# A run-time branch of an expert stage, moved ahead of the last products of two expert pairs

## The chip, the core and the metric

The kernel runs on one core of a Trainium2 chip. Its time is the device time of one execution in microseconds (us); several executions are timed and their median is given. Engines are named as in the profile: PE multiplies matrices (PEld loads its stationary operand), DVE and ACT work on vectors, POOL is the fourth engine, and SP issues most of the loads. Each engine runs its own list of instructions in order; they meet through semaphores. All loads of weights go from HBM through 16 DMA engines.

## What is computed

The program computes two transformer blocks on 256 tokens of width 1024. The part that matters here is the last one, a mixture of experts: each token goes to 2 of 16 experts, and each expert has a hidden width of 512.

```python
def hier_moe(h, w_rg, b_rg, w_re, b_re, w1, w3, w2):
    ...
    def expert_step(acc, xs):
        w1e, w3e, w2e, ge = xs
        y = (jax.nn.silu(t @ w1e) * (t @ w3e)) @ w2e
        return acc + ge[:, None] * y, None

    acc, _ = lax.scan(expert_step, jnp.zeros_like(t), (w1, w3, w2, gates))
    return acc.reshape(b, n, d)
...
        x_lat = x_lat + g2 * hier_moe(h2_l, ...)
    return rmsnorm(x_lat, final_g)
```

## The kernel before

The kernel is one long program that a scheduler has put in order; the expert stage at its end is written in a fixed order (a manual schedule for PE; the others follow the order of the code). It takes the experts in 8 pairs; pair p is the experts 2p and 2p+1, each on 64 of PE's 128 columns. Every expert has 64 places for tokens. Tokens are gathered into these places by products with one-hot matrices (`gather`, for two pairs at a time) and brought back in the same way (`back` transposes the one-hot matrix, `scatter` and its `add` multiply with it and add to x).

For each pair the loop in `_body` (from `for p in range(8)`, L2051) issues on PE:

- `gate(p)`: the product with the pair's gate weights into `pg`; ACT makes `hp` of it (L1908, Silu).
- `down(p - 1)`: the product of the pair before with its down weights into two halves of `yacc`; `scatter(p - 1)` then has DVE multiply each half into `yf` (L1938), ACT round it to `yh` (L1939), and DVE keep the rest in `yl` (L1940).
- `up(p)`: the product with the up weights into `pu`; DVE multiplies it into `hp` (L1913).
- `back(p)`: two transposes (L1883), which DVE copies to `back` (L1884).
- `add()`: the products with `yh` and `yl` of the pair before (L1946, L1947), which DVE adds to x (L1948).
- `hidden_T`: four transposes of `hp` (L1920), which ACT copies to `hT` (L1921), the operand of `down(p)`.

The weights come as f32 in pieces of 1 MB, four for each product. `load_rows` (L250) issues them on SP into 14 buffers used in turn (`rawa`, `raw`, `rawb` and the tile `K01`, which the profile prints as K). A load waits until the products that read its buffer before are done, and until the load that used the same one of eight semaphores (DMAHW0 to DMAHW7, in turn) has landed. A product waits for the semaphore of each piece. In the text (7,0), (7,1) and (7,2) are the four loads of pair 7's gate, up and down weights; (6,2) are those of pair 6's down weights.

If an expert gets more than 64 tokens, a general path (`overflow`) computes the excess. Whether it is needed is known only at run time: the count `novi` is read into a register on every engine (L1960), and every engine branches on it (L1961). With the inputs used here the path is not taken. The path uses the tiles `yf`, `yh`, `hp`, `hT` and `few` of the pool that `scatter` uses too (four buffers of 128x1024 in turn), and ACT issues its loads into `few`. Where it is not taken, each engine adjusts its own semaphores as if it had been: it waits until its semaphore has reached the value that it has before the branch, and adds what the path would have added. SP does this for DMAHW0 to DMAHW7, one after the other.

In the kernel before, the branch stands in the last turn of the loop, behind `hidden_T` of pair 7 and ahead of `down(7)`. Just ahead of it the four loads of (7,2) are issued, so that they are in the queue when SP comes to the branch. After the loop follow `down(7)`, the scatter of pair 7, and the final normalisation (from L2076).

Of the kernel before, what the change touches and what calls it, by code (L numbers as in the profile page):

```python
# [117 lines left out]
def _body(tc, nc, es, I, out, dbg, stop, R):  # L118
# [28 lines left out]
    def alloc(kind, w, name, dt, tag=None):  # L147
        if kind == "2" and P.get("ffn2"):
            return a2(name, dt)
        t = (P["tag"].get(P["s"], P["s"]) if tag is None else tag) + kind  # L150
        if t not in P["b"]:
            t = kind
        return P["pool"].tile([128, w], dt, name=name, tag="k" + t, bufs=P["b"][t])

    def t4(name, dt=F32, tag=None):
        return alloc("4", 1024, name, dt, tag)
# [14 lines left out]
    def pa(name):  # L171
        t = pp.tile([128, 512], F32, name=name, tag="A", bufs=4)
        return t
# [11 lines left out]
    def pc2(name, t=None):  # L185

        if t is None:
            P["n2"] += 1
            t = "CD"[P["n2"] % 2]
        if P["pairs"]:  # L190
            t = pc(name, t)
            return [t[:, 0:512], t[:, 512:1024]]
        return [P["psum"].tile([128, 512], F32, name=name, tag=f"{t}{n}", bufs=1) for n in range(2)]
# [17 lines left out]
    def f32(ap):  # L211
        return ap.bitcast(F32)
# [25 lines left out]
    def load_rows(src, k):  # L238

        n, i = R["raws"], nraw[0] % sum(R["raws"])  # L240
        if i < n[0]:
            raw = P["raw1"].tile([128, 2048], F32, name="rawa", tag="rawa", bufs=n[0])
        elif i < n[0] + n[1]:
            raw = raw_tile()
        elif i == sum(n) - 1:
            raw = K01
        else:
            raw = P["raw2"].tile([128, 2048], F32, name="rawb", tag="rawb", bufs=n[2])
        nraw[0] += 1
        nc.sync.dma_start(raw, src.rearrange("(p k) n -> p (k n)", k=k))  # L250
        return raw
# [1446 lines left out]
    for i in range(4):  # L1698
# [5 lines left out]
        for f in range(2):  # L1704
            k, yf = 2 * i + f, ya[:, 256 * f:256 * f + 256]
# [172 lines left out]
    def back(p):  # L1878

        t = backs[p] = t1("back", F32R)  # L1880
        ps = pa("oht")
        for b in range(2):
            PE.transpose(ps[:, 128 * b:128 * b + 128], f32(oh[b][:, 128 * p:128 * p + 128]), ident)  # L1883
        DVE.tensor_copy(t, ps[:, 0:256])  # L1884
# [6 lines left out]
    ahead = {}  # L1891

    def fetch(p, i):
        n = 512 if i < 2 else 256
        return [[load_rows(experts[i][2 * p + u][n * h:n * h + n], n // 128) for u in range(2)] for h in range(2)]

    def product(p, i, ps):
        raws = ahead.pop((p, i), None) or fetch(p, i)
        for h, raw in enumerate(raws):
            for j in range(4):  # L1900
                k = 4 * h + j
                pair_mm(ps, xe[p](k), [r[:, 512 * j:512 * j + 512] for r in raw], k == 0, k == 7)

    def gate(p):
        ps = pa("pg")
        product(p, 0, ps)
        hps[p] = alloc("h", 512, "hp", F32, "")
        ACT.activation(hps[p], ps, AF.Silu)  # L1908

    def up(p):  # L1910
        ps = pa("pu")
        product(p, 1, ps)
        DVE.scalar_tensor_tensor(hps[p], ps, gsl[:, p:p + 1], hps[p], op0=OP.mult, op1=OP.mult)  # L1913

    def hidden_T(hp, t):

        ps = pa("eT")
        for f in range(4):
            o = 256 * (f // 2) + f % 2
            PE.transpose(ps[:, 128 * f:128 * f + 128], hp[:, o:256 * (f // 2) + 256:2], ident)  # L1920
        ACT.activation(t, ps, AF.Copy)  # L1921
        return t

    def down(p):
        yaccs[p] = pc2("yacc")
        raws = ahead.pop((p, 2), None) or fetch(p, 2)
        steps = [(f, n) for f in range(4) for n in range(2)]
        if p == 7:
            steps[4:] = [(2, 0), (3, 0), (2, 1), (3, 1)]
        for f, n in steps:  # L1930
            o = 1024 * (f % 2) + 512 * n
            pair_mm(yaccs[p][n], hTs[p][:, 128 * f:128 * f + 128], [r[:, o:o + 512] for r in raws[f // 2]], f == 0, f == 3)

    def scatter(p):

        yf, yh_, yl_ = t4("yf"), t4("yh", F32R), t4("yl", F32R)
        for n in range(2):
            tt(part(yf, n), yaccs[p][n], part(g2b, n), op=OP.mult)  # L1938
            ACT.activation(part(yh_, n), part(yf, n), AF.Copy)  # L1939
            tt(part(yl_, n), part(yf, n), f32(part(yh_, n)), op=OP.subtract)  # L1940

        def add():
            for n in range(2):
                for b in range(2):
                    r, ps = backs[p][:, 128 * b:128 * b + 128], pa("scat")
                    mm(ps, r, part(yh_, n), start=True, stop=False)  # L1946
                    mm(ps, r, part(yl_, n), start=False, stop=True)  # L1947
                    tt(part(x[b], n), part(x[b], n), ps, op=OP.add)  # L1948

        return add  # L1950

    def overflow():

        def some(w, k, i, n):

            t = t4("few")
            nc.scalar.dma_start(t.rearrange("p (k n) -> p k n", k=n), w.rearrange("(p k) n -> p k n", k=k)[:, i:i + n])
            return t

        nov = nc.values_load(novi, min_val=0, max_val=512)  # L1960
        with tc.If(nov > 0):  # L1961
            e_ = mybir.EngineType
            with tc.manual_schedule(engines={e_.PE, e_.DVE, e_.Activation, e_.Pool, e_.SP}):
                for b in range(2):
                    t, xT = t4("yf"), t4("yh")
                    tt(t, f32(xnh[b]), f32(xnl[b]), op=OP.add)
                    for k in range(8):
                        ps = pa("gat")
                        PE.transpose(ps[:, 0:128], t[:, 128 * k:128 * k + 128], ident)
                        DVE.tensor_scalar(xT[:, 128 * k:128 * k + 128], ps[:, 0:128], sc2p[:, k:k + 1], sh2p[:, k:k + 1],  # L1970
                                          op0=OP.mult, op1=OP.add)
                    acc = pc2("yacc")
                    for e in range(16):
                        hp = part(t4("hp"), 0)
                        for i in range(2):
                            ps = pa("pg")
                            for k in range(8):
                                if k % 2 == 0:
                                    raw = some(experts[i][e][512 * (k // 4):512 * (k // 4) + 512], 4, k % 4, 2)
                                mm(ps, xT[:, 128 * k:128 * k + 128], part(raw, k % 2), start=k == 0, stop=k == 7)  # L1980
                            if i:
                                DVE.scalar_tensor_tensor(hp, ps, gov[:, b, e:e + 1], hp, op0=OP.mult, op1=OP.mult)
                            else:
                                ACT.activation(hp, ps, AF.Silu)
                        hT = hidden_T(hp, part(t4("hT"), 0))
                        for f in range(4):
                            raw = some(experts[2][e][256 * (f // 2):256 * (f // 2) + 256], 2, f % 2, 1)
                            for n in range(2):
                                mm(acc[n], hT[:, 128 * f:128 * f + 128], part(raw, n), start=e + f == 0, stop=e == 15 and f == 3)
                    t = t4("yf")  # L1990
                    for n in range(2):
                        tt(part(t, n), acc[n], part(g2b, n), op=OP.mult)
                        tt(part(x[b], n), part(x[b], n), part(t, n), op=OP.add)
# [55 lines left out]
    with tc.manual_schedule(engines={mybir.EngineType.PE}):  # L2049
        add = None  # L2050
        for p in range(8):  # L2051
            gate(p)
            if p:
                down(p - 1)
                add = scatter(p - 1)
            else:
                places()
            up(p)
            if p % 2 and p < 7:
                gather(p + 1)  # L2060
            back(p)
            if add:
                add()
            hTs[p] = hidden_T(hps[p], alloc("h", 512, "hT", F32, ""))
            if p == 7:
                ahead[7, 2] = fetch(7, 2)
                overflow()
        down(7)
        scatter(7)()

# [66 lines left out]
```

## Time and profile before

| | us |
|---|---|
| median of 3 runs | 1166.79 |
| lowest and highest run | 1160.59, 1168.51 |
| the profiled execution | 1166.33 |
| its span, first to last instruction | 1164.6 |
| PE busy in the span | 1099.5 (94%) |
| DVE busy | 656.5 (56%) |
| ACT busy | 513.0 (44%) |
| POOL busy | 61.9 (5%) |
| mean granted clock of PE | 0.98 |

The times of the rows below are those of the profiled execution, in us from the start of its span. A row of a timeline has the start, the duration, the engine, the line, the operation, what it writes and reads, shapes, and the number of instructions merged in it; in brackets stands the idle time of the engine before it and what ended it. A "q" behind an engine's name is its sequencer, which waits, branches and issues.

### The profile page before, as it was taken

Reading aid. Unit: us, or ns where it says so; the run is one execution under the profiler, and the core shown is the slowest. Engines: PE = TensorE matmul, PEld = TensorE weight load, DVE = VectorE, ACT = ScalarE, POOL = GpSimd, SP = SyncE. Lnnn points to the kernel's source line nnn. Section 1 sums busy time; section 2 is a strip of 40 time slices with the busy share of each in tenths; the row PEclk is TensorE's granted clock in tenths of the full one; section 3 lists DMA queues with packets and bytes.
Section 4 is the critical chain, followed back from the end, with each engine's and each line's share of the span. In section 5 each row is a group of like instructions: output and inputs, shape, how many; then the busy total and the mean of one; then the engine's idle time right before and its main releaser. Section 6 shows DMA issues by size and latency. Waiting matters only on the chain. (4 is left out here: it accounts for less than half of the span.)

```text
span 1164.6 us, 16858 instructions
## 1 busy us (share of the span) xinstructions
PE 1099.5 (94%) x6823; PEld 834.5 (72%) x6823; DVE 656.5 (56%) x1050; ACT 513.0 (44%) x847; POOL 61.9 (5%) x106
## 2 busy tenths in 40 slices
PE   6999999998988999999999999999899899999994
PEld 5888887987765787888888688888799734343432
DVE  5656666555886566666566775656646603332323
ACT  5555554575563355555555444655544400100002
POOL 1000001000230011000000100000000300000000
PEclk9999999998999999999999999999999899999997
DMA  9855654553466737655565555313385699999992
GB/s 327 296 190 182 207 187 148 164 168 112 149 232 226 232 127 275 212 183 180 187 210 189 166 179 163 109 55 113 113 314 188 250 371 420 422 420 420 421 421 102
DMA packets 119534, 262.90 MB, mean 226 GB/s; under 512 B 6873, under 2 KB 83802, under 8 KB 105242
## 3 DMA queue, kind: packets, MB, share of 16 engines
q1 hardware_dynamic: 118506, 258.88, 61.8%
q0 software_dynamic: 656, 2.36, 0.5%
q8 instruction: 55, 0.90, 0.3%
q10 hardware_dynamic: 288, 0.52, 0.1%
q14 instruction: 29, 0.24, 0.1%
HBM read 260.70 MB, written 1.05 MB: 225 GB/s over the span
## 5 line engine op out<-in xcount | busy, mean ns | idle before, releaser
L268 DVE TENSOR_TENSOR lo<-raw,hi 128x1024 fp32r<-128x1024 f32 x243 | 297.2, 1224 | 213.7 <-ACT hi L267 213.4
L267 ACT ACTIVATE hi<-raw 128x1024 fp32r<-128x1024 f32 x246 | 260.2, 1058 | 213.5 <-PE pj L230 66.5
L308 PE MATMUL pj<-H,hi 128*128 128x512 f32 x352 | 122.1, 396 | 0.4 <-DVE H L599 0.4
L308 PE MATMUL pj<-hT,hi 128*128 128x512 f32 x352 | 122.0, 394 | 0.5 <-DVE hT L538 0.5
L229 PE MATMUL pj<-H,hi 128*128 128x256 f32 x400 | 117.6, 294 | 0.0
L231 PE MATMUL pj<-H,lo 128*128 128x256 f32 x400 | 113.6, 284 | 0.0
L230 PE MATMUL pj<-H,hi 128*128 128x256 f32 x400 | 113.6, 284 | 0.0
L311 PE MATMUL pj<-hT,lo 128*128 128x256 f32 x352 | 91.6, 281 | 0.0
L311 PE MATMUL pj<-H,lo 128*128 128x256 f32 x352 | 91.5, 281 | 0.0
L229 PEld LDWEIGHTS pj<-H,hi 128*128 128x128 f32 x400 | 76.9, 192 | 7.5 <-issue 4.4
L230 PEld LDWEIGHTS pj<-H,hi 128*128 128x128 f32 x400 | 76.9, 192 | 0.5 <-issue 0.5
L231 PEld LDWEIGHTS pj<-H,lo 128*128 128x128 f32 x400 | 76.8, 192 | 0.4 <-issue 0.3
L308 PEld LDWEIGHTS pj<-hT,hi 128*128 128x128 f32 x352 | 63.6, 188 | 13.3 <-DVE hT L538 1.5
L308 PEld LDWEIGHTS pj<-H,hi 128*128 128x128 f32 x352 | 64.1, 190 | 12.4 <-DVE H L599 0.8
L311 PEld LDWEIGHTS pj<-H,lo 128*128 128x128 f32 x352 | 66.8, 190 | 3.9
L311 PEld LDWEIGHTS pj<-hT,lo 128*128 128x128 f32 x352 | 66.2, 188 | 4.1
L1938 DVE TENSOR_TENSOR yf<-yacc,K 128x512 f32<-128x512 f32 x16 | 11.1, 691 | 100.0 <-PE yacc L1889 100.0
L423 PE MATMUL acc<-hi,hTh 128*128 128x512 f32 x160 | 62.7, 392 | 0.0
L424 PE MATMUL acc<-lo,hTh 128*128 128x512 f32 x160 | 62.7, 392 | 0.0
L427 PE MATMUL acc<-hi,hTl 128*128 128x512 f32 x160 | 49.8, 392 | 0.0
L1921 ACT ACTIVATE hT<-eT 128x512 f32<-128x512 f32 x8 | 4.8, 597 | 93.3 <-PE eT L1920 93.3
L647 ACT ACTIVATE gs<-pj 128x256 f32<-128x256 f32 x44 | 16.9, 384 | 44.3 <-PE pj L308 44.2
(518 smaller groups left out, 2113.2 us busy)
## 6 DMA issues: line engine op xcount, KB each, us to landing
raw<-in_w_in_dram SPq DMA_DIRECT2D x43, 1024.0 KB, 5.2
raw<-in_ffn_up_dram SPq DMA_DIRECT2D x22, 1024.0 KB, 5.5
raw<-in_ffn_down_dram SPq DMA_DIRECT2D x22, 1024.0 KB, 5.0
raw<-in_ffn_gate_dram SPq DMA_DIRECT2D x21, 1024.0 KB, 5.3
raw<-in_w_mod_dram SPq DMA_DIRECT2D x15, 1024.0 KB, 5.2
rawa<-in_w_exp_gate_dram SPq DMA_DIRECT2D x14, 1024.0 KB, 15.3
rawa<-in_w_exp_up_dram SPq DMA_DIRECT2D x11, 1024.0 KB, 13.2
raw<-in_w_exp_up_dram SPq DMA_DIRECT2D x11, 1024.0 KB, 19.8
```

Source lines behind the costliest of these rows:

```text
L229: mm(o, l[0], r[0], start=first, stop=False)
L230: mm(o, l[0], r[1], start=False, stop=False)
L231: mm(o, l[1], r[0], start=False, stop=last)
L267: ACT.activation(hi, r, AF.Copy)
L268: low = lambda: (sub or DVE).tensor_tensor(lo, r, f32(hi), op=OP.subtract)
L308: high = lambda: mm(ps, wh[:, s_], hl2(k), start=k == 0, stop=k == 7)
L311: mm(ps[:, 0:256], wl[:, s_], hl2.h(k), start=False, stop=False)
L423: mm(ps[b][n], hh, wh[:, s_], start=first and f == 0, stop=False)
L424: mm(ps[b][n], hh, wl[:, s_], start=False, stop=False)
L427: mm(ps[b][n], ll, wh[:, s_], start=False, stop=last and f == 1)
L647: ACT.activation(t, a, AF.Copy)
L1938: tt(part(yf, n), yaccs[p][n], part(g2b, n), op=OP.mult)
```

## The change

The branch and the loads move to an earlier place in the last turn of the loop: behind `gate(7)`, ahead of `down(6)` and `up(7)`. Since all loads issued later than the branch would come behind it in SP's list, the loads of (6,2) and (7,1) are issued ahead of it too, by a table that `down` and `product` read (`ahead`). Nothing else is changed.

```diff
         for p in range(8):
             gate(p)
+            if p == 7:
+
+                ahead.update({k: fetch(*k) for k in ((6, 2), (7, 1), (7, 2))})
+                overflow()
             if p:
                 down(p - 1)
                 add = scatter(p - 1)
...
             hTs[p] = hidden_T(hps[p], alloc("h", 512, "hT", F32, ""))
-            if p == 7:
-                ahead[7, 2] = fetch(7, 2)
-                overflow()
         down(7)
         scatter(7)()
```

On PE the branch stands, in the kernel before, behind the transposes `eT` of pair 7; L1969 is the general path's first instruction:

```order
L1946 MATMUL scat<-yh,back 128x512 [waits DVE_49]
L1947 MATMUL scat<-yl,back 128x512
L1920 MATMUL eT<-ident,hp 128x128 [waits DVE_49]
L1920 MATMUL eT<-ident,hp 128x128 x3
L1960 TENSOR_LOAD novi [waits DVE_49]
L1961 COMPARE_AND_BRANCH
L1969 MATMUL gat<-ident,yf 128x128 [waits DVE_49]
```

In the changed kernel it stands on PE behind the last products `pg` of pair 7's gate:

```order
L1889 MATMUL pg<-K_79,xe 64x512
L1889 MATMUL pg<-rawb,xe 64x512
L1889 MATMUL pg<-K_79,xe 64x512
L1960 TENSOR_LOAD novi [waits DVE_49]
L1961 COMPARE_AND_BRANCH
L1969 MATMUL gat<-ident,yf 128x128 [waits DVE_49,PE_49,Activation_49]
```

So the products of down(6) and up(7), the transposes of the one-hot matrix, the eight scatter products of pair 6 and the four transposes `eT` have moved from ahead of the branch to behind it.

On DVE, in the kernel before, the whole scatter of pair 6 stands ahead of the branch, and `yf` of that pair waits for PE alone:

```order
L1938 TENSOR_TENSOR yf<-yacc,K_81 128x512 [waits PE_49] x2
L1940 TENSOR_TENSOR yl<-yf,yh 128x512 [waits Activation_49] x2
L1913 SCALAR_TENSOR_TENSOR hp<-pu,gsl,hp 128x512 [waits PE_49]
L1884 CAST back<-oht 128x256 [waits PE_49]
L1948 TENSOR_TENSOR x_70<-x_70,scat 128x512 [waits PE_49]
L1948 TENSOR_TENSOR x_72<-x_72,scat 128x512 [waits PE_49]
L1948 TENSOR_TENSOR x_70<-x_70,scat 128x512 [waits PE_49]
L1948 TENSOR_TENSOR x_72<-x_72,scat 128x512 [waits PE_49]
L1960 TENSOR_LOAD novi [waits DVE_49]
L1961 COMPARE_AND_BRANCH
```

In the changed kernel the same rows of DVE stand behind the end of the general path (its two last branches are the first rows here):

```order
L1961 UNCONDITIONAL_BRANCH
L1961 UNCONDITIONAL_BRANCH [waits DVE_49]
L1938 TENSOR_TENSOR yf<-yacc,K_81 128x512 [waits DMAHW3_49,DMAHW4_49,DMAHW1_49,DMAHW5_49,DVE_49,DMAHW6_49,PE_49,Activation_49]
L1938 TENSOR_TENSOR yf<-yacc,K_81 128x512 [waits PE_49]
L1940 TENSOR_TENSOR yl<-yf,yh 128x512 [waits DMAHW6_49,DMAHW3_49,Activation_49]
L1940 TENSOR_TENSOR yl<-yf,yh 128x512 [waits Activation_49]
L1913 SCALAR_TENSOR_TENSOR hp<-pu,gsl,hp 128x512 [waits PE_49]
L1884 CAST back<-oht 128x256 [waits PE_49]
L1948 TENSOR_TENSOR x_70<-x_70,scat 128x512 [waits PE_49]
L1948 TENSOR_TENSOR x_72<-x_72,scat 128x512 [waits PE_49]
```

The first `yf` behind the branch takes on waits for five of the eight load semaphores; the first `yh` behind it, on ACT, waits for all eight. In the program built from the changed kernel the value that `yf` asks of DMAHW6 is 1264; each load adds 16, the 34 loads on that semaphore reach 544, and SP's adjustment at the branch adds 768. In the kernel before, the same waits stand at `yf` and `yh` of pair 7. On SP the rows are the same in both kernels.

## Rows read from the trace of the kernel before

**Rows 1.** The page, the span in 40 equal slices.

```profile
DMA  9855654553466737655565555313385699999992
GB/s 327 296 190 182 207 187 148 164 168 112 149 232 226 232 127 275 212 183 180 187 210 189 166 179 163 109 55 113 113 314 188 250 371 420 422 420 420 421 421 102
```

**Rows 2.** Stretches: length, busy us of PE, PEld, DVE, ACT, POOL; clock; DMA; GB/s.

```profile
1135.50:1138.30 2.80, 2.77 (x15) 2.23 (x14) 2.69 (x5) 0.00 (x0) 0.00 (x0) 1.00 1.01 418
1138.30:1142.50 4.20, 0.00 (x0) 0.00 (x0) 0.78 (x2) 0.60 (x1) 0.00 (x0) 0.99 0.43 174
1142.50:1146.00 3.50, 3.46 (x10) 1.22 (x12) 0.00 (x0) 0.00 (x0) 0.00 (x0) 0.53 0.03 7
```

**Rows 3.** Timeline of PE around the branch.

```profile
1137.64 0.63 PE L1920 MATMUL eT<-ident,hp 128*128 128x128 f32 x4
1142.55 1.08 PE L1889 MATMUL yacc<-raw,hT 128*64 128x512 f32 x1 [4.27 <-PEq L1961]
...
1143.42 1.06 PE L1889 MATMUL yacc<-raw,hT 128*64 128x512 f32 x1
...
1147.20 4.03 PE L1889 MATMUL yacc<-rawb,hT 128*64 128x512 f32 x17
```

**Rows 4.** The branch's lines, every engine: durations in ns min/median/max, first and last start.

```profile
L1961 SPq EVENT_SEMAPHORE  x8: 17/17/17, 1126.9 to 1141.9; - x8
...
L1961 SPq COMPARE_BRANCH  x1: 45/45/45, 1122.9 to 1122.9; - x1
L1961 PEldq COMPARE_BRANCH  x1: 4287/4287/4287, 1137.9 to 1137.9; - x1
...
L1961 ACTq COMPARE_BRANCH  x1: 50/50/50, 1138.8 to 1138.8; - x1
...
L1961 ACTq EVENT_SEMAPHORE  x1: 17/17/17, 1141.7 to 1141.7; - x1
...
L1960 PEldq TENSOR_LOAD <-novi x1: 488/488/488, 1137.3 to 1137.3; - x1
```

**Rows 5.** SP's last three loads: their issue; KB each, median us to landing.

```profile
1117.01 5.31 SPq L250 DMA_DIRECT2D rawb<-in_w_exp_down_dram  x3
...
rawb<-in_w_exp_down_dram SPq DMA_DIRECT2D x3, 1024.0 KB, 19.8
```

**Rows 6.** Timeline of PE: first and last row of gate(7), the end of up(7).

```profile
1110.62 4.08 PE L1889 MATMUL pg<-rawb,xe 128*64 128x512 f32 x17
...
1117.12 0.59 PE L1889 MATMUL pg<-K,xe 128*64 128x512 f32 x1
...
1131.93 3.65 PE L1889 MATMUL pu<-raw,xe 128*64 128x512 f32 x14 [1.33 <-SPq L1961]
```

**Rows 7.** Timeline of ACT: hT of pair 7.

```profile
1138.31 0.60 ACT L1921 ACTIVATE hT<-eT 128x512 f32<-128x512 f32 x1 [11.30 <-PE eT L1920]
```

**Rows 8.** Timelines of DVE, PE and ACT: from hp to hT of pair 6.

```profile
1108.07 0.75 DVE L1913 SCALAR_TENSOR_TENSOR hp<-pu,gsl,hp 128x512 f32<-128x512 f32 x1 [4.79 <-PE pu L1889]
...
1109.07 2.47 DVE L1948 TENSOR_TENSOR x<-x,scat 128x512 f32<-128x512 f32 x4
...
1110.06 0.63 PE L1920 MATMUL eT<-ident,hp 128*128 128x128 f32 x4
...
1110.73 0.60 ACT L1921 ACTIVATE hT<-eT 128x512 f32<-128x512 f32 x1 [8.17 <-PE eT L1920]
```

**Rows 9.** DVE and ACT, scatter of pair 6, then of pair 7; DVE's events at yf.

```profile
1124.79 0.69 DVE L1938 TENSOR_TENSOR yf<-yacc,K 128x512 f32<-128x512 f32 x1 [13.25 <-PE yacc L1889]
...
1149.61 0.69 DVE L1938 TENSOR_TENSOR yf<-yacc,K 128x512 f32<-128x512 f32 x1 [10.52 <-PE yacc L1889]
1150.99 0.69 DVE L1940 TENSOR_TENSOR yl<-yf,yh 128x512 fp32r<-128x512 f32 x1 [0.70 <-ACT yh L1939]
...
1150.33 0.63 ACT L1939 ACTIVATE yh<-yf 128x512 fp32r<-128x512 f32 x1 [11.43 <-DVE yf L1938]
...
L1938 DVEq EVENT_SEMAPHORE  x4: 21/50/7695, 1139.2 to 1141.9; - x4
```

## Prediction

> **What bounds the kernel now.** I read the page's slices first, then the end of the kernel in stretches, then the timelines of each engine around the branch, and last the rows of the branch line itself. A busy PE tells little here; the DMA row tells more: it stands at 9 tenths and about 420 GB/s from slice 33 to slice 39, and only the last slice falls to 102 GB/s [rows 1]. So the expert stage runs at the pace of its loads, and what can be won there is what stands after the last load. [...]
>
> The gap is the branch. PE's timeline has the last transposes of pair 7 at 1137.64 to 1138.27, then nothing until the first product of down(7) at 1142.55, an idle time of 4.27 us put down to PE's own sequencer at L1961; after it the first pair of matmuls takes 0.87 us (1142.55 to 1143.42), and down(7)'s last matmul ends at 1151.23, 13.4 us before the span's end [rows 3]. The branch line explains it: PE's compare-and-branch lasts 4.29 us. The same table has eight semaphore events on SP that run from 1126.9 to 1141.9 [rows 4]. They matter below.
>
> **What the change moves, part by part.**
>
> The loads. SP's list holds the same loads in the same order before and after: (7,0), (6,2), (7,1), (7,2), then the branch. The last three are issued from 1117.01 on and take 19.8 us to land; the third of them is issued at 1122.0 (the row's end, 1122.3, less one issue of 0.3), so it lands at 1141.8 [rows 5]. They wait for buffers that gate(7) and earlier products free, all ahead of either place of the branch. Nothing is gained or lost here: 0 us.
>
> The branch on PE. [...] Where it goes away it gives back the gap, up to the wait that is next: hT(7) on ACT would end at 1138.91 [rows 7], and down(7) could start at about 1139.0. Where it is added, behind it stand down(6), up(7), the back transposes, the scatter products of pair 6 and the transposes of pair 7. At most it costs 4.4 us of gap and the 1.6 us that down(7) pays now for the low clock (1142.55 to 1151.23 is 8.68 us, against 7.1): down(6) from 1122.1 to 1130.8, up(7) to 1137.9. At least it costs nothing, because the sequencer can run ahead of the array: in [rows 4] its load of the count starts at 1137.3, before the transposes that stand ahead of it have started at 1137.64. Both ends lie before 1144.6, where up(7)'s result is first wanted (next part), so I take 0 us in either case. The cover is that wait; without it the upper end would be 2.4 us, since up(7) now ends at 1135.6 [rows 6].
>
> The branch on ACT and DVE. ACT's takes 2.9 us (1138.8 to its event at 1141.7) [rows 4] and would come behind Silu(7), some 0.7 us after the end of gate(7) at 1117.71: done by about 1121.5, before anything needs ACT. DVE's comes behind the adds that end at 1111.54 [rows 8]; if it took ACT's 2.9 us, it would be past before gate(7) ends. 0 us for both.
>
> The correction of the semaphores. This is the part that decides. A branch that isn't taken must leave every semaphore where the taken one would leave it. SP does that for the eight load semaphores: it waits until each has counted all loads issued before the branch, in the order 0 to 7, and adds what the path not taken would have added. That is why its eight events end at 1141.9, with the last landing [rows 4]. Whatever comes behind the branch and reuses a buffer of the general path waits for the corrected values. The order shows which: yf on DVE waits for semaphores 3, 4, 1, 5 and 6, yh on ACT for all eight. In the kernel before, these were yf and yh of pair 7, which had to wait for down(7) anyway: DVE's four events at yf lie from 1139.2 to 1141.9 and the last one, 7.7 us long, then waits for PE [rows 9]. In the changed kernel the first to reuse such a buffer is yf of pair 6. It starts now at 1124.79 [rows 9]; semaphore 6 is corrected at 1141.8, so it will start at about 1141.95, some 17 us later.
>
> Behind yf on DVE are queued, strictly in turn, the second yf, two yl, the product hp(7) with the gate, the cast of back(7) and the four adds. PE's scatter products wait for yh and yl, its transposes of pair 7 for hp, ACT's hT for them, and down(7) for hT. The sum from 1141.95, each step by the rows of before:
> - yf to yh 0.72, yh to yl 0.66 (1149.61, 1150.33, 1150.99) [rows 9]; the second yf fills in, yh follows it, and the second yl starts at 1143.95; a DVE operation of this size starts 0.6 after the one before it (four adds in 2.47 us, [rows 8]), so hp starts at 1144.57.
> - [...] But PE will have idled from the end of up(7) to the first yh, some 6 to 8 us, longer than the 4.27 us after which it is granted 0.53 now. [...] I take the low clock here, because this is a longer idle time followed by thinner work than in [rows 2]: 1148.9.
> - down(7): 0.07 to its start, 7.1 at full clock, 8.68 with a whole low stretch like now. I take one slow pair, 7.5: the end at 1156.5. Bounds: 1155.0 (full clock throughout) and 1157.7 (the low stretch of now again).
> - The 13.4 us behind it are unchanged: the same rows in the same order, and pair 6's adds, done by about 1149, are out of the way.
>
> The end of down(7) moves from 1151.23 to 1156.5: **+5.3 us**, between +3.8 and +6.5. The profiled execution took 1166.33 us around a span of 1164.6, so 1171.6; the median of the three runs is 1166.79, 0.46 above it, which I don't add since the runs lie between 1160.59 and 1168.51. I forecast 1171.5 us.
>
> **The rivals.**
>
> *Faster: the corrected values don't hold the scatter.* If yf(6) runs when down(6) is done, as now, only the gap goes: down(7) starts at 1139.0, its second half needs the load of 1141.8 at about 1142.5, and it ends at 1146.1 instead of 1151.23: -5.1 us, 1161.2 us. For it speaks that SP passes its own compare already at 1122.9 [rows 4] and that the products themselves wait only for their own loads. Against it: the waits stand in the order, DVE's four events at yf are in the trace of before, and the value for semaphore 6 can't be reached by loads alone. It decides from the point where semaphore 6 is corrected before about 1124.8, which needs the last load 17 us earlier. [...]
>
> *Much slower: the branch in the middle of saturated loads.* At 1117 up to eight loads are queued, where at 1138 two were left. If the fetch at the branch's target had to wait behind all of them, it would return some 20 us later (the 19.8 us of [rows 5]), at about 1139.6; then down(6) 8.7, up(7) 7.1, 3.3 to hT and down(7) 7.1 follow: 1165.8, +14.6 us, 1180.9 us. For it: both share the DMA engines. Against it: PE's branch took 4.29 us although DMA still moved at 418 GB/s until 1138.3 and 174 GB/s on average after it [rows 2]. It decides from a fetch longer than about 11 us; shorter ones hide in the wait for yf(6). [...]
>
> **How the numbers follow.** The wait for the corrected semaphores is written in the program, and the rows give every step behind it: 0.86. The faster rival 0.08, the much slower one 0.06. About 1%, 11.7 us, is what a measurement of this kernel can tell from no change. The forecast with its +3.8 to +6.5 lies within it, as does the faster rival; the scatter of the runs (7.9 us from lowest to highest) puts a little of each over the edge. So faster by over 1% 0.02, within 1% 0.89, slower 0.09, most of that from the second rival. The range is 1171.5 with its bounds, 1170.1 to 1172.8, widened by the scatter of the runs on both sides: 1165.0 to 1177.0, which leaves out both rivals.
>
> **What would show it.** Right: in the changed kernel DVE's yf(6) starts within 0.3 us of the last of SP's eight events, near 1142; PE has no gap over 1 us between gate(7) and down(6) or one that ends before up(7) is wanted, but one of 5 to 8 us between the back transposes and the first scatter product, with the low clock behind it; down(7) starts near 1149 and the span ends near 1170. Wrong: yf(6) near 1125 and a span near 1159.5 (the first rival), or PE's compare-and-branch over 11 us (the second). If the gap behind the back transposes is there but down(7) starts before 1147, the step on the low clock was wrong.

## The result and the profile after

The changed kernel takes 1171.91 us (median of 15 runs, 1170.43 to 1177.03), the kernel before, run beside it, 1167.71 us (15 runs, 1160.24 to 1170.49). The ratio is 1.0057, with a 95% interval of 1.0040 to 1.0073: 6.7 us more (1167.7 times 0.0057), between 4.7 and 8.5. The ratio is an estimate from all runs; the two medians alone differ by 4.2 us (1.0036), the two means by 6.1 (1.0052). That is a loss, and a small one, as forecast. The profiled execution took 1171.76 us around a span of 1170.0.

The two profiled executions don't start the expert stage's end at the same time: hp of pair 6, which stands ahead of everything that was moved, starts at 1108.07 before [rows 8] and at 1106.76 after. So I count from there to the end of the span: 56.5 us before, 63.2 us after, 6.7 us more.

The branch's lines of the changed kernel, which answer to [rows 4] (durations in ns, first and last start):

```profile
L1961 SPq EVENT_SEMAPHORE  x8: 17/17/17, 1125.6 to 1140.7; - x8
...
L1961 PEldq COMPARE_BRANCH  x1: 6092/6092/6092, 1112.5 to 1112.5; - x1
L1961 ACTq COMPARE_BRANCH  x1: 50/50/50, 1117.1 to 1117.1; - x1
...
L1961 ACTq EVENT_SEMAPHORE  x1: 17/17/17, 1122.1 to 1122.1; - x1
...
  DVE yf L1938: 30.5, 1
...
L1960 PEldq TENSOR_LOAD <-novi x1: 487/487/487, 1112.0 to 1112.0; - x1
```

SP's eight corrections still end with the last load, at 1140.7. New is the row of yf: DVE sat idle 30.5 us ahead of it and was released by this line. The timelines of DVE and ACT, which answer to [rows 7 to 9], show what came of it:

```profile
1106.76 0.75 DVE L1913 SCALAR_TENSOR_TENSOR hp<-pu,gsl,hp 128x512 f32<-128x512 f32 x1 [4.79 <-PE pu L1889]
...
1140.75 1.29 DVE L1938 TENSOR_TENSOR yf<-yacc,K 128x512 f32<-128x512 f32 x2 [30.52 <-SPq L1961]
1142.14 1.29 DVE L1940 TENSOR_TENSOR yl<-yf,yh 128x512 fp32r<-128x512 f32 x2
1143.35 0.74 DVE L1913 SCALAR_TENSOR_TENSOR hp<-pu,gsl,hp 128x512 f32<-128x512 f32 x1
...
1147.18 0.60 ACT L1921 ACTIVATE hT<-eT 128x512 f32<-128x512 f32 x1 [4.47 <-PE eT L1920]
```

yf of pair 6 starts at 1140.75 instead of 1124.79, within 0.1 us of the last correction, and hp(7) stands behind the scatter in DVE's queue: 1143.35 instead of 1135.62. PE's timeline, against [rows 3, 6]:

```profile
1118.96 7.09 PE L1889 MATMUL yacc<-rawa,hT 128*64 128x512 f32 x32 [2.56 <-PEq L1961]
...
1134.31 0.44 PE L1883 MATMUL oht<-ident,oh 128*128 128x128 f32 x2
1142.16 0.80 PE L1946 MATMUL scat<-yh,back 128*128 128x512 f32 x1 [7.41 <-ACT yh L1939]
...
1145.66 0.63 PE L1947 MATMUL scat<-yl,back 128*128 128x512 f32 x1
1146.09 1.05 PE L1920 MATMUL eT<-ident,hp 128*128 128x128 f32 x4
1147.83 1.11 PE L1889 MATMUL yacc<-raw,hT 128*64 128x512 f32 x1 [0.69 <-ACT hT L1921]
...
1151.29 0.63 PE L1889 MATMUL yacc<-raw,hT 128*64 128x512 f32 x1
...
1152.62 4.03 PE L1889 MATMUL yacc<-rawb,hT 128*64 128x512 f32 x17
```

The gap of 4.27 us ahead of down(7) is gone. A gap of 2.56 us stands ahead of down(6) instead, and it is covered. What is not covered is the 7.41 us between the back transposes and the first scatter product. Behind it the eight scatter products follow each other in steps of 0.42 to 0.72 us, and the first four pairs of down(7) in steps of 0.85 to 0.90: down(7) lasts from 1147.83 to 1156.65, 8.82 us. The stretches give the clock (columns as in [rows 2]):

```profile
1135.50:1143.00 7.50, 0.84 (x2) 0.41 (x2) 2.15 (x4) 1.23 (x2) 0.00 (x0) 0.65 0.44 184
1143.00:1149.00 6.00, 5.31 (x15) 3.28 (x17) 3.90 (x7) 0.60 (x1) 0.00 (x0) 0.50 0.01 3
1149.00:1156.50 7.50, 7.50 (x30) 2.06 (x26) 0.77 (x2) 0.63 (x1) 0.00 (x0) 0.84 0.00 0
```

Behind the idle stretch of 7.41 us PE works at a granted clock of 0.50 for all of 1143 to 1149. The end behind down(7) is what it was: 1156.65 to 1170.0, 13.35 us.

### The profile page after: what moved, and what is told of

Read it like the earlier page. It is cut to its first block, busy times and chain, and to the rows that moved or that the text cites. A ratio compares the mean times of both kernels' runs of the same rounds, so it can differ in the third digit from the quotient of the medians.

```text
span 1170.0 us, 16861 instructions
## 1 busy us (share of the span) xinstructions
PE 1101.1 (94%) x6823; PEld 834.9 (71%) x6823; DVE 656.4 (56%) x1050; ACT 513.0 (44%) x847; POOL 62.1 (5%) x106
## 5 line engine op out<-in xcount | busy, mean ns | idle before, releaser
L423 PE MATMUL acc<-hi,hTh 128*128 128x512 f32 x160 | 62.7, 392 | 0.0
L424 PE MATMUL acc<-lo,hTh 128*128 128x512 f32 x160 | 62.7, 392 | 0.0
L1939 ACT ACTIVATE yh<-yf 128x512 fp32r<-128x512 f32 x16 | 10.0, 630 | 71.7 <-DVE yf L1938 71.7
## 6 DMA issues: line engine op xcount, KB each, us to landing
raw<-in_w_exp_up_dram SPq DMA_DIRECT2D x11, 1024.0 KB, 19.8
```

The costliest lines, as they stand in the source:

```text
L423: mm(ps[b][n], hh, wh[:, s_], start=first and f == 0, stop=False)
L424: mm(ps[b][n], hh, wl[:, s_], start=False, stop=False)
```

## The experiments

The theory: yf, yh and yl of pair 6 reuse tiles of the general path and so wait for SP's corrected semaphores; the low clock behind the wait (0.50 from 1143 to 1149) adds to it. The rivals: the branch itself, or its fetch, is what costs at the new place; or the low clock alone. The ratio is to the kernel before, run on the same chip; "from hp(6)" is the span's end less the start of hp(6) in the profiled execution, 56.5 us before.

| kernel | median us (runs) | ratio, 95% interval | from hp(6) |
|---|---|---|---|
| changed | 1171.91 (15) | 1.0057, 1.0040 to 1.0073 | 63.2 |
| changed, again | 1174.45 (10) | 1.0057, 1.0037 to 1.0077 | 60.4 |
| other tiles for pair 6 | 1161.16 (12) | 0.9961, 0.9942 to 0.9980 | 51.7 |
| only yf in another tile | 1170.03 (12) | 1.0032, 1.0015 to 1.0050 | 59.3 |
| no branch | 1161.35 (12) | 0.9961, 0.9941 to 0.9982 | 50.7 |
| loads alone | 1167.36 (12) | 1.0000, 0.9977 to 1.0023 | 55.6 |
| last loads behind the branch | 1167.22 (12) | 0.9989, 0.9969 to 1.0009 | 54.1 |
| branch behind the adds | 1170.84 (10) | 1.0042, 1.0020 to 1.0063 | 59.5 |
| branch behind up(7), other tiles | 1167.99 (12) | 1.0008, 0.9991 to 1.0025 | 60.0 |
| unused products | 1174.22 (6) | 1.0065, 1.0045 to 1.0086 | 60.4 |
| unused products, again | 1173.73 (6) | 1.0061, 1.0037 to 1.0084 | 62.7 |

**Other tiles for pair 6.** The cause itself: everything stays where the change put it, only the tiles differ.

```diff
-        yf, yh_, yl_ = t4("yf"), t4("yh", F32R), t4("yl", F32R)
+        if p == 6:
+            yf, yh_, yl_ = alloc("xe", 2048, "yf", F32, "")[:, :1024], xnh[0], xnl[0]
+        else:
+            yf, yh_, yl_ = t4("yf"), t4("yh", F32R), t4("yl", F32R)
```

> The changed kernel with one thing different: the scatter of pair 6 no longer takes its three tiles from the pool that the general path uses; yf goes into the free third gather tile, yh and yl go over the two tiles of the normalised x that nobody reads behind the branch. The branch stays behind gate(7). Theory (yf(6) is held by SP's corrected semaphores because of the shared tiles): yf(6) starts right behind down(6), near 1125 us, the gap of PE behind the back transposes falls to under 1 us, down(7) starts near 1139 and ends near 1146 instead of 1151.2 in the kernel before: 5.1 us less than the kernel before, ratio 0.9956 (0.994 to 0.998), and some 10 to 11 us less than the changed kernel. Rival (the price is the branch itself and its fetch at a place where the loads are saturated): as the changed kernel, ratio 1.0057. Rival (only the low clock costs): as the changed kernel within 2 us.

The ratio is 0.9961, within the expected 0.994 to 0.998. The timelines of DVE and PE of this kernel:

```profile
1128.45 0.69 DVE L1941 TENSOR_TENSOR yf<-yacc,K 128x512 f32<-128x512 f32 x1 [16.72 <-PE yacc L1889]
...
1120.48 8.78 PE L1889 MATMUL yacc<-rawa,hT 128*64 128x512 f32 x32 [2.59 <-PEq L1964]
...
1132.11 4.03 PE L1889 MATMUL pu<-raw,xe 128*64 128x512 f32 x17
...
1138.21 0.63 PE L1920 MATMUL eT<-ident,hp 128*128 128x128 f32 x4
1139.53 0.64 PE L1889 MATMUL yacc<-raw,hT 128*64 128x512 f32 x1 [0.69 <-ACT hT L1921]
...
1142.59 4.03 PE L1889 MATMUL yacc<-rawb,hT 128*64 128x512 f32 x17
```

yf now waits for PE, not for SP, and it runs while down(6) ends. The gap behind the back transposes is gone, down(7) starts at 1139.53 and runs at full clock (1.00 from 1136.5 to 1146.6). The branch still costs its gap of 2.59 us ahead of down(6), and down(6) even runs slow (8.78 us, with a clock of 0.91 from 1118 to 1136.5), and neither shows in the time, as the kernel without a branch tells below. So the held tiles are the loss, about 11 us of it (1.0057 less 0.9961, times 1167). This version is faster than both kernels.

**Only yf in another tile.** Is it enough to move the instruction that waits first?

```diff
-        yf, yh_, yl_ = t4("yf"), t4("yh", F32R), t4("yl", F32R)
+        yf, yh_, yl_ = alloc("xe", 2048, "yf", F32, "")[:, :1024] if p == 6 else t4("yf"), t4("yh", F32R), t4("yl", F32R)
```

> The changed kernel with only yf of pair 6 in the free gather tile; yh and yl stay in the pool that the general path uses. It tells whether moving the first waiting instruction is enough. Theory (every reuse of a tile of that pool waits, yh on ACT for all eight semaphores): yf runs right behind down(6), near 1125, but yh starts only with the last correction near 1140.7, yl 0.7 later, and hp(7) stands behind yl in DVE's queue: hp(7) near 1142.6 instead of 1143.35, at most 1 us less than the changed kernel, ratio to the kernel before 1.004 to 1.006. Rival (the wait of yf on DVE is the only one that counts): as the kernel with all three tiles moved, 0.9961.

Measured 1.0032 (1.0015 to 1.0050), a little under the expected 1.004 to 1.006 and far from the rival's 0.9961. The timelines of DVE and ACT show the wait one instruction further on:

```profile
1127.90 0.69 DVE L1938 TENSOR_TENSOR yf<-yacc,K 128x512 f32<-128x512 f32 x1 [16.57 <-PE yacc L1889]
...
1141.76 1.29 DVE L1940 TENSOR_TENSOR yl<-yf,yh 128x512 fp32r<-128x512 f32 x2 [12.30 <-ACT yh L1939]
1142.97 0.74 DVE L1913 SCALAR_TENSOR_TENSOR hp<-pu,gsl,hp 128x512 f32<-128x512 f32 x1
...
1141.09 1.15 ACT L1939 ACTIVATE yh<-yf 128x512 fp32r<-128x512 f32 x2 [22.89 <-SPq L1961]
```

yh on ACT takes over the wait for SP, 22.89 us, and hp(7) still stands behind yl. So yh carries the wait as yf did; a wait of yl's own can't be told here, since yl follows yh in any case.

**No branch.** The call of `overflow()` is taken out.

```diff
                 ahead.update({k: fetch(*k) for k in ((6, 2), (7, 1), (7, 2))})
-                overflow()
```

> The changed kernel without the branch and the general path behind it, which is left out (the loads stay ahead, in the changed order). It gives the whole price of the branch at either place. Theory: hT(7) ends near 1138.9, down(7) starts near 1139 and ends near 1146.1: 5.1 us less than the kernel before, ratio 0.9956 (0.994 to 0.998), and the same within 1 us as the kernel with other tiles for pair 6. If the branch behind gate(7) costs more than the held tiles, this kernel is faster than the one with other tiles by that price. Rival (the loads set the end, the branch costs nothing): within 1 us of the kernel before.

0.9961, the same as with other tiles. The whole price of the branch in the kernel before is thus about 4.6 us (0.0039 times 1167; 2.1 to 6.9 by the interval), and other tiles win all of it that the runs can tell: at its new place the branch costs nothing beyond an interval of 0.2% each way, and about 1 us by the two profiles (51.7 less 50.7). The change as it stands wins the 4.6 us and loses the 11 us of the held tiles: 6.7 us more.

**The loads alone.** The other part of the change by itself.

```diff
             if p == 7:
                 ahead.update({k: fetch(*k) for k in ((6, 2), (7, 1), (7, 2))})
-                overflow()
...
             hTs[p] = hidden_T(hps[p], alloc("h", 512, "hT", F32, ""))
+            if p == 7:
+                overflow()
```

> One part of the change alone: the three fetches (6,2), (7,1), (7,2) stand together behind gate(7), as in the changed kernel, and the branch stays at its old place behind the transposes of pair 7. Theory: the list of loads is the same, so nothing moves: ratio 0.999 to 1.001 to the kernel before. Rival (fetching ahead itself costs, by the order of tiles or by semaphores): slower by up to the 0.57% of the change.

1.0000 (0.9977 to 1.0023): the loads cost nothing, within 0.23%.

**The last loads behind the branch.** This shortens the wait without touching the tiles.

```diff
-                ahead.update({k: fetch(*k) for k in ((6, 2), (7, 1), (7, 2))})
+                ahead.update({k: fetch(*k) for k in ((6, 2), (7, 1))})
                 overflow()
```

> The changed kernel with the loads of (7,2) issued behind the branch; (6,2) and (7,1) stay ahead of it. SP then corrects its semaphores when the last load of (7,1) has landed, and issues (7,2) only after that. Theory: yf(6) starts near 1131 instead of 1140.8, so that hp(7) and hT(7) come right behind up(7); what is late next is the last load of (7,2), which lands 13 to 15 us after the correction, near 1144 to 1146, and down(7)'s second half waits for it: down(7) ends near 1148 to 1149, 2 to 3 us before that of the kernel before, ratio 0.9975 (0.996 to 1.000). Rival (the place of the branch is the price): as the changed kernel, ratio 1.0057.

The ratio is 0.9989 (0.9969 to 1.0009): inside the expected span and 0.7% below the changed kernel, but not shown to be faster than the kernel before. The rows of the branch line, SP, DVE and PE:

```profile
L1961 SPq EVENT_SEMAPHORE  x8: 17/17/17, 1129.9 to 1135.2; - x8
...
1112.30 0.75 DVE L1913 SCALAR_TENSOR_TENSOR hp<-pu,gsl,hp 128x512 f32<-128x512 f32 x1 [4.79 <-PE pu L1889]
...
1135.66 0.34 SPq L250 DMA_DIRECT2D raw<-in_w_exp_down_dram  x1
...
1135.36 1.29 DVE L1938 TENSOR_TENSOR yf<-yacc,K 128x512 f32<-128x512 f32 x2 [19.59 <-SPq L1961]
...
1149.34 3.65 PE L1889 MATMUL yacc<-rawb,hT 128*64 128x512 f32 x14 [1.31 <-DMA rawb<-in_w_exp_down_dram]
```

yf follows the last correction again. It starts 23.1 us after hp(6) (1112.30), against 34.0 in the changed kernel (1106.76 to 1140.75): the wait moves with the corrections. What is late next is the last load, which SP could issue only behind them: down(7)'s second half waits for it until 1149.34.

**The branch behind the adds.** A third place, where pair 6 is through. (The branch's old place, behind `hidden_T`, is empty.)

```diff
             up(p)
             if p % 2 and p < 7:
                 gather(p + 1)
-            back(p)
+            if p < 7:
+                back(p)
             if add:
                 add()
+            if p == 7:
+                ahead[7, 2] = fetch(7, 2)
+                overflow()
+                back(p)
```

> The branch at a third place: behind up(7) and the adds of pair 6, ahead of the back transposes and the transposes of pair 7; the loads are issued ahead of it in the order of the kernel before. Theory: nothing of pair 6 waits for corrected semaphores here, so yf(6) runs near 1125; PE's branch of 4.3 us begins while up(7)'s last products and the eight scatter products are still pending, so that part of it is covered; down(7) starts between 1139.5 and 1141.5 instead of 1142.55 with a shorter idle time of PE ahead of it: 1 to 4.5 us less than the kernel before, ratio 0.996 to 0.999. Rival (the branch costs its 4.3 us on the path wherever it stands close to the end): the same as the kernel before, ratio 0.9995 to 1.0005. Rival (the branch is dearer while loads are saturated): slower, 1.001 to 1.005.

1.0042 (1.0020 to 1.0063): slower than before, a miss. It lies in the range of the last rival, but not by its mechanism: PE's compare began when the loads were ending, and its 4.49 us are hardly more than the 4.29 of before. PE's timeline, hp(7) on DVE, and the branch's lines:

```profile
1136.15 0.39 PE L1947 MATMUL scat<-yl,back 128*128 128x512 f32 x1
1140.76 0.41 PE L1883 MATMUL oht<-ident,oh 128*128 128x128 f32 x2 [4.22 <-PEq L1961]
1143.76 1.01 PE L1920 MATMUL eT<-ident,hp 128*128 128x128 f32 x4 [2.59 <-issue]
...
1134.54 0.75 DVE L1913 SCALAR_TENSOR_TENSOR hp<-pu,gsl,hp 128x512 f32<-128x512 f32 x1 [7.88 <-PE pu L1889]
...
L1960 PEldq TENSOR_LOAD <-novi x1: 505/505/505, 1135.3 to 1135.3; - x1
...
L1961 PEldq COMPARE_BRANCH  x1: 4487/4487/4487, 1136.0 to 1136.0; - x1
```

PE read the count only at 1135.3, with 1.2 us of products left, so its 4.2 us are bare here. I put that down to the scatter products ahead of the branch: their result tiles are used in turn with the one of up(7), which hp(7) frees at 1135.29 in this profile. Then comes a second pause of 2.59 us ahead of the transposes, for which the profile shows no releaser. Between 1134 and 1148 the queue that the profile lists as q8, instruction, has three packets where the kernel before and the loads alone have two; that this makes the pause is not shown. So its cause is open. Both stand on the path here, since hp(7) had long been done.

**The branch behind up(7), with other tiles.** To have products left that cover the branch.

```diff
             up(p)
+            if p == 7:
+                ahead[7, 2] = fetch(7, 2)
+                overflow()
```

(The tiles of pair 6 as in the first experiment, the branch's place behind `gate(7)` empty.)

> The branch directly behind up(7), ahead of the back transposes and of the adds of pair 6, with the scatter of pair 6 in other tiles as before (yf in the free gather tile, yh and yl over the normalised x). In the kernel with the branch behind the adds, PE read the count only at 1135.3, when hp(7) was done, and then stood 4.2 us. Theory (PE's sequencer is held there by the scatter products, whose result tiles come free only with hp(7); it runs some 17 products ahead where nothing holds it): here PE reads the count while 14 or more products of up(7) are pending, near 1131, its compare ends near 1136, and the gap ahead of the back transposes is 1 to 2 us instead of 4.2; the total is 2 to 4 us less than the kernel before, ratio 0.9965 to 0.9985, or 2.6 us more than that if the pause of 2.6 us ahead of the transposes of pair 7 comes again. Rival (the branch costs its 4.3 us behind the last product wherever it stands late): 1.000 to 1.004.

1.0008 (0.9991 to 1.0025) instead of 0.9965 to 0.9985: a miss, and within the rival's range. The branch line and PE's timeline:

```profile
L1963 PEldq TENSOR_LOAD <-novi x1: 503/503/503, 1136.0 to 1136.0; - x1
...
L1964 PEldq COMPARE_BRANCH  x1: 6067/6067/6067, 1136.6 to 1136.6; - x1
...
1135.91 3.65 PE L1889 MATMUL pu<-raw,xe 128*64 128x512 f32 x14 [1.31 <-SPq L1964]
1142.96 0.66 PE L1883 MATMUL oht<-ident,oh 128*128 128x128 f32 x2 [3.40 <-PEq L1964]
```

PE did read the count with 14 products still to run, but only once the wait for up(7)'s last load was over, at 1135.9. They cover 3 us, the compare lasts 6.07, and 3.40 us are left. Here the sequencer that runs ahead stopped at the wait for a load (1.31 us of idle time on PE ahead of 1135.91; the count is read at 1136.0). (This profiled execution, 1172.58 us, was the slowest of the twelve, so its steps don't add up to the median.)

**Unused products on PE.** What is the low clock worth?

```diff
+    def warm(n):
+        ps = pa("warm")
+        for _ in range(n):
+            mm(ps, xnh[0][:, 0:128], xnh[0][:, 0:512], start=True, stop=True)
...
             back(p)
+            if p == 7:
+                warm(30)
```

> The changed kernel with 30 products that nobody uses (128x512, on the normalised x) on PE between the back transposes of pair 7 and the scatter of pair 6, where PE idles 7.4 us. It tells what the low clock is worth behind the wait. Theory: the wait for SP's corrected semaphores stays (yf(6) near 1140.8, the first scatter product near 1142.2), but the scatter products take 0.23 us each instead of 0.43, the transposes 0.6 instead of 1.05 and down(7) 7.1 instead of 8.8: 2.5 to 4 us less than the changed kernel, 2.5 to 4 us more than the kernel before, ratio to it 1.002 to 1.0035. Rival (the low clock costs nothing that ends last): as the changed kernel, 1.0057. Rival (the low clock is the whole loss): as the kernel before or faster, 1.000.

The ratio, 1.0065, was that of the changed kernel, though the profile looked like a gain. So both ran again side by side:

> The changed kernel itself once more, on the same chip as the next one, so that the two stand side by side. Expected ratio to the kernel before 1.004 to 1.0073, as in its first timing.

> The kernel with 30 unused products once more, beside the changed kernel. Its profile showed down(7) at full clock (7.0 us) and 26.7 us from yf(6) to the end of the span against 29.25 in the changed kernel, but its six timed runs gave 1.0065. Theory (the low clock costs 2.6 us): 2 to 3 us below the changed kernel of this call, ratio to the kernel before about 1.003. Rival (the unused products cost elsewhere what they give back here, as by a lower clock ahead of the end): no difference to the changed kernel.

1.0057 and 1.0061: no difference, and both kernels with unused products miss the gain that was expected of them. PE's timeline of the second profile of the changed kernel tells why the first comparison misled:

```profile
1145.06 0.79 PE L1946 MATMUL scat<-yh,back 128*128 128x512 f32 x1 [7.39 <-ACT yh L1939]
...
1148.43 0.40 PE L1947 MATMUL scat<-yl,back 128*128 128x512 f32 x1
...
1149.98 0.64 PE L1889 MATMUL yacc<-raw,hT 128*64 128x512 f32 x1 [0.69 <-ACT hT L1921]
...
1153.04 4.03 PE L1889 MATMUL yacc<-rawb,hT 128*64 128x512 f32 x17
```

It is the same program with the same wait (7.39 us), but the slow stretch ends within the scatter products, and down(7) takes 7.09 us (1149.98 to 1157.07, at a clock of 1.00 from 1150 to 1157.2) instead of 8.82. From yf(6), at 1143.65 here, to the end of the span it is 26.9 us instead of 29.25: the low clock is worth 2.4 us more or less from one execution to the next, without any edit. And in the kernel with unused products it came back (second profile):

```profile
1135.47 7.10 PE L1955 MATMUL warm<-H 128*128 128x512 f32 x30
1143.64 0.50 PE L1946 MATMUL scat<-yh,back 128*128 128x512 f32 x1 [1.07 <-ACT yh L1939]
...
1145.63 0.79 PE L1946 MATMUL scat<-yh,back 128*128 128x512 f32 x1 [0.76 <-DVE hp L1913]
...
1147.93 0.63 PE L1947 MATMUL scat<-yl,back 128*128 128x512 f32 x1
```

The unused products also take a result tile, so that the third scatter product now waits for hp. What the low clock costs on the average is thus not settled. In both profiles of the changed kernel it stands behind the wait; with other tiles for pair 6, where that wait is gone, down(7) runs at full clock (1.00) in the one profile there is.

## Why the prediction was right

The forecast was 1171.5 us, the median is 1171.91; +5.3 us by the steps, +6.7 (4.7 to 8.5) by the ratio and +4.2 by the medians. That the two times agree within 0.4 us is partly luck: the kernel before, on whose 1166.33 us the forecast was built, came out at 1167.71 beside the changed one. The mechanism is what the forecast said it was. Point by point:

- *The loads, 0 us.* Right: the loads alone give 1.0000, and the last correction lies 33.9 us behind hp(6) in the changed kernel (1140.7 less 1106.76) against 33.8 before.
- *The branch on PE, 0 us behind the cover of the wait for hp(7).* Right in the sum, and the gap of 2.56 us lies within the 0 to 4.4 that were taken; the reason was only part of it. The cover was to be the wait for hp(7), without which up to 2.4 us would come through. With other tiles that wait is gone, and still only about 1 us comes through by the profiles (51.7 against 50.7 without a branch). What covers the gap first is up(7): before, it pauses twice for its loads, 1.32 us ahead of 1126.94 and 1.33 ahead of 1131.93 (the second in [rows 6]); with the branch in front and other tiles it runs through without a pause, its last 17 products from 1132.11 on. It ends 27.5 us behind hp(6) before, 27.6 in the changed kernel and 27.9 with other tiles. The sequencer runs ahead, as taken: it reads the count at 1112.0, 4 us before gate(7)'s last products. The branch itself was undersized: PE's compare lasts 6.09 us, not 4.29. Had only the branch's gap counted, the change would have gained the faster rival's 5.1 us; the wait for the tiles took that gain and more.
- *The branch on ACT and DVE, 0 us.* Right in the sum: nothing waits for either. DVE was past it at 1110.3. ACT's took 5.0 us (1117.1 to 1122.1) where the forecast took 2.9 from the kernel before: it was past it 15.3 us behind hp(6), and not 13.4.
- *The corrected semaphores hold yf(6).* Right, and shown twice: by moving the tiles, and by moving the corrections, which yf followed to 1135.36 (the last one there is at 1135.2). The forecast had yf start 33.9 us behind hp(6); it is 34.0. The value of 1264 that yf waits for stands in the program and in no trace; the traces show that yf starts with the last correction.
- *yf to hp, 2.62 us.* 2.60.
- *hp to the end of hT, 4.36 us with 1.1 us for the low clock.* The steps are 1.99, 0.67 and 0.60 us [rows 8] and an estimate of 1.1, from a pair of matmuls of 0.87 us [rows 3] where gate(7) takes 0.44 for each of its 16 (7.1 us in all, [rows 6]). No run shows the 1.1 by itself; the whole took 4.43 in the first profile and 3.7 in the second (1146.25 to 1149.93).
- *down(7), 7.5 us with one slow pair.* The term that was mis-sized: 8.82 in the first profile, with four slow pairs, and 7.09 in the second, with none. The bounds, 7.1 and 8.68, are nearly the two lengths that occurred; the value between them occurred in neither. The end of the low stretch shifts against the work from one profile to the other (1151.29 against 1148.43, 9.1 and 3.4 us behind the first scatter product), so it had to be a range.
- *The tail, 13.4 us.* 13.35.

The span from hp(6) is 6.7 us longer in the first profile and 3.9 in the second; the forecast of +5.3 lies between them. The faster rival, 1161.2, is what the kernel would have given with its own tiles for pair 6: 1161.16 measured (a ratio of 0.9961; that the times agree to 0.04 us is luck). Its products were ready, as it said; what it overlooked is who held the tiles. The much slower rival did not occur: PE's compare lasted 6.09 us while DMA moved 415 GB/s (1112.5 to 1118.6), where it would have needed over 11. That instructions come over the DMA engines too, which spoke for it, the profile shows: in that stretch it has two packets of instruction queues beside 344 of the loads' queue. But a small part of what it says may be in the 1.8 us above 4.29 (last section). The rival's time doesn't follow from the rows: the end of gate(7), 1117.71, and 19.8 us give 1137.5 and not 1139.6, so 1178.8 us and not 1180.9; both lie outside the range. And the 1% that the forecast took as the least that a measurement can tell is too much: the interval of these runs, 1.0040 to 1.0073, tells 0.57% from nothing. Two readings are off without weight: slice 33 stands at 371 GB/s and not at about 420 [rows 1], and 1137.9 less 1135.6 is 2.3 and not 2.4.

## What to carry to other kernels

A branch at run time can cost more than its own gap: here the gap was 2.56 us, and the held tiles about 11. In this program, where the path not taken would have loaded into shared tiles, what reuses those tiles behind the branch waits until the loads issued ahead of the branch have landed. So before a branch is moved earlier, look at what stands behind it in the same pool, and give the next users other tiles. Here that turned a loss of 0.57% into a gain of 0.39%, with the branch at the very same place.

## What the hardware showed beside

PE's compare-and-branch has two lengths here: 4.29, 4.63 and 4.49 us (before; loads alone; behind the adds), and 5.96 to 6.11 us in seven others (changed, twice; other tiles; only yf; last loads behind; behind up(7); unused products). ACT's has two as well, from its compare to its next event: 2.9 and 3.0 us (before; loads alone), and 5.0 to 5.4 in those seven and behind the adds. In the kernel with the branch behind the adds ACT's is a long one and PE's a short one. The stretches of the two show what differs (columns as in [rows 2]):

```profile
1125.80:1131.20 5.40, 4.00 (x18) 1.38 (x20) 0.76 (x2) 0.13 (x1) 0.00 (x0) 1.00 1.00 416
1136.00:1140.50 4.50, 0.54 (x3) 0.12 (x1) 1.69 (x3) 0.00 (x0) 0.00 (x0) 1.00 0.64 266
```

So it is in the two kernels of the forecast: the long ones of the changed kernel ran at a DMA share of 1.02 (1112.5 to 1118.6 on PE, 1117.1 to 1122.1 on ACT), the short ones of the kernel before at 0.51 and 0.44 (1137.9 to 1142.2, 1138.8 to 1141.7). And in all ten profiles each long one, on PE and on ACT, began 9 us or more ahead of SP's last correction, which comes with the last landing, and each short one less than 5 us ahead of it. On PE the long ones also began with a dozen products or more still to run, the short ones with hardly any; ACT, which had at most one operation running when any of its branches began, speaks for the loads. A run that changes the loads alone was not made, so the cause stays open. Either way PE's branches amid loads were the longer ones here (5.96 to 6.11 us against 4.29 to 4.63), and running ahead hid less than the short length would suggest: 2.56 us of gap stayed with nearly 4 us of products still to come.

And two executions of one program, both with an idle time of 7.4 us on PE, came back to full clock at different points: 9.1 us behind the first scatter product in one (1142.16 to 1151.29, at 0.50; then 0.99 up to 1156.5), 3.4 us in the other (1145.06 to 1148.43; 1.00 from 1150 to 1157.2). A single profile is no measure of what the low clock costs.
